# Recurrence on quarters of the array, u tiles two steps ahead, a third one-hot buffer: one change to a two-layer encoder on one core

## The chip, the core and the metric

The kernel runs on one core of a Trainium2 chip. The core has five engines that work side by side: TensorE (in profiles PE, and PEld for its weight loads), VectorE (DVE), ScalarE (ACT), GpSimd (POOL) and SyncE (SP), and 16 DMA engines. Each engine takes its instructions in the order in which the program issues them and waits on semaphores for what other engines must have done. The metric is the device time of one execution in microseconds. The number that counts is the median of several runs, and beside it stands one execution that the hardware profiler recorded.

## What is computed

Two residual layers over 512 tokens of 1,024 channels, everything in fp32. Layer 0 mixes with stick-breaking attention and pooling; layer 1 mixes with forgetting attention and with a recurrence; after each mixer comes an expert layer. Two parts matter here.

The recurrence has 8 heads of width 64:

```python
def step(state, inp):
    r_t, w_t, k_t, v_t, kk_t, a_t = inp
    sa = jnp.einsum('bhvk,bhk->bhv', state, kk_t)
    state = (state * w_t[:, :, None, :] - sa[..., None] * (kk_t * a_t)[:, :, None, :]
             + v_t[..., None] * k_t[:, :, None, :])
    y = jnp.einsum('bhvk,bhk->bhv', state, r_t)
    return state, y
```

The expert layer has 16,384 experts, each with one vector u and one vector v. Every token chooses 16 of them in each of 8 heads:

```python
s1 = jnp.einsum('thd,nd->thn', q[:, :, 0], sub_k1); v1, i1 = lax.top_k(s1, PEER_TOPK)
...
top_s, pos = lax.top_k(cand.astype(jnp.float32), PEER_TOPK)
gate = jax.nn.softmax(top_s, axis=-1)
act = jax.nn.gelu(jnp.einsum('thkd,td->thk', expert_u[ib], xb), approximate=False)
out = jnp.einsum('thk,thkd->td', gate * act, expert_v[ib])
```

## The kernel before

`build` runs `even_mixer`, `peer` (layer 0), `odd_mixer`, `peer` (layer 1). The order of the work on each engine is the order in which the Python code issues it; generators are advanced by hand to weave one piece of work into another. Nothing reorders it later. A tile that is taken again from a pool of `bufs` buffers waits until the last user of the buffer's former tile is done.

**The recurrence** (end of `odd_mixer`, lines 1094 to 1275) works on 8 chunks of 64 tokens. Within a chunk the recurrence is written as matrix products, with the inverse of a 64x64 triangular matrix for every head. The 8 heads are held as 4 pairs: partitions 0 to 63 carry one head of the pair, 64 to 127 the other. `expand` (line 718) spreads such a pair into a 128x128 block whose two diagonal quarters are the two heads and whose other quarters are zero, by multiplying with a mask; it runs on POOL, for chunk 0 partly on VectorE and ScalarE. `mm4` (line 1114) multiplies four such blocks, one for each pair, into one PSUM bank. `prep(c)` (line 1118) makes, for one chunk, the expanded operands, completes the inverse `XT` from 16 to 32 to 64 rows (masks `level`, products with N1 and N2), and turns k, b and v. It needs nothing of the state and is woven in as the preparation of the next chunk. `step(c)` (line 1187) has the chain that goes from state to state: psT, evicted as t1 by ScalarE; psU, evicted as u; psS, which with the decayed old state `se` makes the new state on VectorE, one operation for each pair; psY, the output. `group_norm(g)` (line 1227) norms two finished chunks with products of full 128x128 blocks, in six pieces woven into the steps of chunks 2 to 7 (the last of it after the loop). The last line of the loop for chunk c drains what is left of the preparation of c+1.

The stage before it computes, between the projections for the attention, the products of `gram` (line 729), one chunk at a time, with an expanded block on one side.

**The expert layer** (`peer`). TensorE multiplies every expert's u with 384 of the 512 tokens and keeps only what the gates choose; the other 128 tokens gather their experts' rows with DMAs. The u matrix comes in 128 tiles of 128 experts. `u_fetch` (line 1358) issues the DMA on SP into one of three buffers `ur`; `u_load` (line 1363) fetches two and makes the high part `uh` on ScalarE; `u_low` (line 1372) makes the low part `ul` on VectorE; `u_mm` (line 1379) does the 24 products (lines 182 to 184 in `mm3`) and the GELU. The first 15 activations stay in the on-chip memory (`NB_ACT`), the next 38 (`NB_SPILL`) are written to HBM and read again by `a_load`. While queries are projected (`for m in range(16)`), the first three tiles are loaded and two of them split, from m = 10 on.

Then `background()` issues the top-16 search and the gates: for every block of 16 tokens VectorE compares and multiplies one-hot rows `ohC`, `ohA` and two `ohB` (line 1606), and `flush` lets TensorE multiply them (line 1589). A block's last flush stands on TensorE behind the operations for the block two later. Costs are added up, and whenever they reach `G_STEP`, `u_step` (line 1626) is issued:

```python
def u_step(j):
    u_low(j + 1)
    u_load(j + 2)
    u_mm(j, j >= NB_ACT)
```

After the gates come the last u products before the v products; then a loop over the 128 v tiles, which first reads spilled activations and, from j = `NB_SPILL` on, does the remaining u products one a turn.

Of the kernel before, what the change touches and what calls it, by code (L numbers as in the profile page):

```python
# [25 lines left out]
P = 128  # L26
# [67 lines left out]
for _nm, _c in (("blk64", 128), ("mB", 128), ("mK", 256), ("lv16", 128), ("lv32", 128), ("hm", 2), ("rows", 4)):  # L94
    OC[_nm] = (_n, _c)
    _n += _c
# [3 lines left out]
def odd_const_array():  # L100
# [12 lines left out]
    put("mK", np.concatenate([same & (rr < qq), same & (rr <= qq)], 1))  # L113
    put("lv16", same & (rr // 32 == qq // 32) & (rr % 32 < 16) & (qq % 32 >= 16))
    put("lv32", same & (rr < 32) & (qq >= 32))
    put("hm", np.stack([i < 64, i >= 64], 1))
# [550 lines left out]
def odd_mixer(k):  # L667
# [8 lines left out]
    with ExitStack() as st:  # L676
# [40 lines left out]
        hm = o_("hm")  # L717

        def expand(e, dst, src):

            if e is nc.scalar:
                for h in range(2):
                    k.act(dst[:, :, 64 * h:64 * h + 64], src, AF.Copy, scale=hm[:, h:h + 1])
                return
            e.tensor_tensor(dst.rearrange("p a (h t) -> p a h t", h=2), src[:, :, None, :].to_broadcast([P, 4, 2, 64]),
                            hm[:, None, :, None].to_broadcast([P, 4, 2, 64]), op=ALU.mult)

        def gram(c, pb):
            tt = slice(64 * c, 64 * c + 64)
            b0 = pb.tile([P, 4, P], F32, name="b0", tag="b0", bufs=2)  # L730
            expand(nc.gpsimd, b0, be[:, :, tt])

            def rest():
                ps = bank4()
                for p in range(4):
                    mm(ps[:, p, :], b0[:, p, :], AR[:, p, :, tt], start=True, stop=True, skip_group_check=True)
                for p in range(4):
                    nc.vector.tensor_tensor(Na[:, :, :, 4 * c + p].rearrange("p i b -> p b i"),
                                            ps[:, p, 0:64].rearrange("p (b i) -> p b i", b=4),
                                            o_("mB")[:, 0:64].rearrange("p (b i) -> p b i", b=4), op=ALU.mult)  # L740
                nc.vector.tensor_tensor(Nr[:, c], ps[:, :, 64:], o_("mB")[:, None, 64:].to_broadcast([P, 4, 64]), op=ALU.mult)
# [5 lines left out]
        with ExitStack() as s1:  # L747
# [136 lines left out]
            with ExitStack() as s2:  # L884
# [40 lines left out]
                def grams(n):  # L925
                    if n >= 4:
                        gq.pop(0)()
                    if 2 <= n < 10:
                        gq.append(gram(n - 2, p3))
# [28 lines left out]
        def bc4(a):  # L958
            return a[:, None, :].to_broadcast([P, 4, P])

# [150 lines left out]
        def t4(nm, n=1, bufs=2):  # L1111
            return pw.tile([P, 4, n * P], F32, name=nm, bufs=bufs)

        def mm4(ps, l, r, start, stop):
            for p in range(4):
                mm(ps[:, p, :], l[:, p, :], r[:, p, :], start=start and p == 0, stop=stop, skip_group_check=True)  # L1116

        def prep(c):
            tt = slice(64 * c, 64 * c + 64)
            K0, B0 = t4("k0"), t4("b0")  # L1120
            AR0 = t4("ar", 2)
            X, XT = t4("x"), t4("xt")
            N1, N2 = t4("n1"), t4("n2", bufs=1)
            NB2 = t4("nb2")

            def level(dst, nm):
                for h in range(2):
                    f = slice(64 * h, 64 * h + 64)
                    (nc.vector if h and not c else nc.gpsimd).tensor_tensor(dst[:, :, f].rearrange("p a (b i) -> p a b i", b=4),
                                            Na[:, :, :, 4 * c:4 * c + 4].rearrange("p i b a -> p a b i"),  # L1130
                                            o_(nm)[:, None, f].rearrange("p a (b i) -> p a b i", b=4)
                                            .to_broadcast([P, 4, 4, 16]), op=ALU.mult)

            ve, ae = (nc.gpsimd, nc.gpsimd) if c else (nc.vector, nc.scalar)
            level(N1, "lv16")
            expand(ve, X, Xc[:, 4 * c:4 * c + 4, :])
            expand(ae, K0, ka[:, :, tt])
            expand(ve, XT, XTc[:, 4 * c:4 * c + 4, :])
            expand(nc.gpsimd, B0, be[:, :, tt])
            yield  # L1140
            expand(ae, AR0[:, :, 0:P], AR[:, :, 0, tt])
            level(N2, "lv32")
            expand(ve, NB2, Nr[:, c])
            expand(nc.gpsimd, AR0[:, :, P:], AR[:, :, 1, tt])
            KT, NT, VT = t4("kt"), t4("nt"), t4("vt")
            ps = bank4()
            for p in range(4):
                for s in range(2):
                    mm(ps[64 * s:64 * s + 64, p, :], vT[:, p, tt], ident, start=True, stop=True, skip_group_check=True)
            nc.vector.tensor_tensor(VT, ps, bc4(cst(k, "blk")), op=ALU.mult)  # L1150

            KK = t4("kk", 2)
            ps = bank4()
            for p in range(4):
                mm(ps[:, p, :], K0[:, p, :], AR[:, p, :, tt], start=True, stop=True, skip_group_check=True)
            for i in range(2):
                nc.vector.tensor_tensor(KK[:, :, i * P:i * P + P].rearrange("p a (h t) -> p a h t", h=2),
                                        ps[:, :, None, 64 * i:64 * i + 64].to_broadcast([P, 4, 2, 64]),
                                        o_("mK")[:, None, i * P:i * P + P].rearrange("p a (h t) -> p a h t", h=2)
                                        .to_broadcast([P, 4, 2, 64]), op=ALU.mult)  # L1160
            ps = bank4()
            mm4(ps, N1, X, True, True)
            Q = t4("q")
            k.act(Q, ps, AF.Copy)
            yield
            ps, ps2 = bank4(), bank4()
            mm4(ps, XT, Q, True, True)
            nc.vector.tensor_tensor(X, X, ps, op=ALU.subtract)
            mm4(ps2, Q, XT, True, True)
            nc.vector.tensor_tensor(XT, XT, ps2, op=ALU.subtract)  # L1170
            yield
            ps = bank4()
            mm4(ps, N2, X, True, True)
            Q = t4("q")
            k.act(Q, ps, AF.Copy)
            for src, dst, sgn in ((K0, KT, 1.0), (B0, NT, -1.0)):
                ps = bank4()
                for p in range(4):
                    nc.tensor.transpose(ps[:, p, :], src[:, p, :], ident)
                k.act(dst, ps, AF.Copy, scale=sgn)  # L1180
            yield
            ps = bank4()
            mm4(ps, Q, XT, True, True)
            nc.vector.tensor_tensor(XT, XT, ps, op=ALU.subtract)
            C[c] = (AR0, KK, KT, NT, VT, XT, NB2)

        def step(c):
            AR0, KK, KT, NT, VT, XT, NB2 = C.pop(c)
            tt = slice(64 * c, 64 * c + 64)
            s0 = S.get(c - 1)  # L1190
            psT = bank4()
            mm4(psT, KK[:, :, 0:P], VT, True, c == 0)
            if c:
                mm4(psT, AR0[:, :, 0:P], s0, False, True)
            t1 = t4("t1", bufs=1)
            k.act(t1, psT, AF.Copy)
            psS, psY = bank4(), bank4()
# [853 lines left out]
```

## Time and profile before

| | us |
|---|---|
| median of 3 runs | 3352.92 |
| lowest and highest run | 3352.59, 3361.28 |
| profiled execution | 3354.57 |
| its span | 3352.8 |
| first gates with u products, 405 to 685 | 280 |
| recurrence, 1861 to 1990 | 129 |
| second gates with u products, 2172 to 2451 | 279 |

A page of the profile gives for each engine the time in which it was busy, and groups of instructions by line, operation and tile. Matmul records are pipelined, so the time from one start to the next is the pace, not the duration of one record; an fp32 product is two records. "128\*128 128x512" reads: a stationary operand of 128 rows and 128 columns, and a moving operand of 128 partitions with 512 columns. In a bracket stands how long the engine was idle before an instruction and what ended that. Lists in order of time merge equal instructions that follow each other. A view of busy time in stretches gives for each stretch its length, the busy time and count of each engine, the granted clock of TensorE as a share of full speed (PEclk), the share of DMA time and the GB/s.

### The profile page before, as it was taken

The numbers are of one execution on the slowest core, as the hardware profiler recorded it, in microseconds if no ns is written. First come the engines' busy times: TensorE is split into PE (matmuls) and PEld (weight loads), VectorE is DVE, ScalarE is ACT, GpSimd is POOL, SyncE is SP. The second block draws the span as 40 slices with busy tenths as digits, with TensorE's granted clock in tenths as the row PEclk, the third lists the DMA queues.
The fourth block names the chain that finished last, engine by engine and source line by source line (L and its number), as shares of the span: only waits on it lengthen the run. The fifth ranks groups of instructions, "written<-read, shape, count | busy, mean of one in ns | idle before, by whom it ended". The sixth has DMA issues, their size and how long they took to land.

```text
span 3352.8 us, 53012 instructions
## 1 busy us (share of the span) xinstructions
PE 3195.3 (95%) x20560; PEld 2795.9 (83%) x20560; DVE 2462.0 (73%) x4771; ACT 1435.1 (43%) x1998; POOL 990.4 (30%) x785
## 2 busy tenths in 40 slices
PE   7999989999999999998999998989989999999998
PEld 5777888888899999986776897888877899999997
DVE  5246888957788888887565466788957788888886
ACT  3353357743333333334445334357743333333334
POOL 1004200013344444443122634200013344444442
PEclk9999999999999999999999999999999999999999
DMA  8524246699999999994520014246789999999984
GB/s 314 189 104 132 89 137 223 230 307 331 314 347 332 325 329 347 330 315 166 185 73 23 4 45 147 93 134 221 238 289 317 316 342 338 328 323 340 340 315 167
DMA packets 317117, 791.10 MB, mean 236 GB/s; under 512 B 23744, under 2 KB 158272, under 8 KB 304576
## 3 DMA queue, kind: packets, MB, share of 16 engines
q1 hardware_dynamic: 222416, 437.95, 38.2%
q0 software_dynamic: 75008, 274.78, 23.5%
q10 hardware_dynamic: 19440, 74.98, 6.0%
q8 instruction: 161, 2.64, 0.3%
q14 instruction: 92, 0.75, 0.1%
HBM read 713.92 MB, written 73.66 MB: 235 GB/s over the span
## 4 chain that ended last, share of the span: by engine, by line
PE 78%; DVE 9%; DMA 5%; ACT 5%; issue 2%; ACTq 0%; POOL 0%; SPq 0%; DVEq 0%; POOLq 0%
PE o L1701 27%; PE ups L184 9%; PE ups L182 9%; PE ups L183 9%; PE bk L1116 3%; PE bk L182 3%; PE bk L184 3%; PE bk L183 3%; DMA vr<-peer_vp 2%; PE qps L182 2%; PE qps L183 2%; PE qps L184 2%; DVE ul L1376 1%; PE gps L1589 1%; PE adaps L242 1%
## 5 line engine op out<-in xcount | busy, mean ns | idle before, releaser
L184 PE MATMUL ups<-phh,ul 128*128 128x384 f32 x2048 | 697.3, 340 | 48.9 <-DVE ul L1376 48.8
L182 PE MATMUL ups<-phh,uh 128*128 128x384 f32 x2048 | 699.0, 341 | 5.8 <-ACT acts L151 5.8
L1723 POOL DMA_INDIRECT row<-peer_u,xres x256 | 350.1, 1368 | 1173.8 <-PE gps L1589 604.3
L183 PE MATMUL ups<-phl,uh 128*128 128x384 f32 x2048 | 691.9, 338 | 0.0
L151 ACT ACTIVATE vh<-vr 128x1024 fp32r<-128x1024 f32 x254 | 269.7, 1062 | 545.3 <-issue 433.9
L1701 PE MATMUL o<-vh,Hh 128*128 128x512 f32 x1524 | 475.6, 393 | 18.3 <-ACT Hh L151 18.3
L1701 PE MATMUL o<-vh,Hl 128*128 128x512 f32 x1524 | 472.4, 391 | 0.0
L1701 PE MATMUL o<-vl,Hh 128*128 128x512 f32 x1524 | 472.3, 391 | 0.0
L1723 POOL DMA_INDIRECT row<-peer_v,xres x256 | 340.3, 1329 | 409.8 <-DVE xres L1739 314.3
L184 PEld LDWEIGHTS ups<-phh,ul 128*128 128x128 f32 x2048 | 389.6, 190 | 58.8 <-DVE ul L1376 58.8
L176 DVE TENSOR_TENSOR vl<-vr,vh 128x1024 fp32r<-128x1024 f32 x254 | 311.1, 1225 | 125.1 <-ACT vh L151 112.8
L182 PEld LDWEIGHTS ups<-phh,uh 128*128 128x128 f32 x2048 | 390.1, 191 | 12.3 <-ACT acts L151 6.4
L183 PEld LDWEIGHTS ups<-phl,uh 128*128 128x128 f32 x2048 | 389.7, 190 | 5.8
L1701 PEld LDWEIGHTS o<-vh,Hh 128*128 128x128 f32 x1524 | 282.8, 188 | 73.7 <-ACT Hh L151 25.7
L1701 PEld LDWEIGHTS o<-vl,Hh 128*128 128x128 f32 x1524 | 286.8, 188 | 62.8
L1701 PEld LDWEIGHTS o<-vh,Hl 128*128 128x128 f32 x1524 | 286.8, 188 | 61.8
L1376 DVE TENSOR_TENSOR ul<-ur,uh 128x1024 fp32r<-128x1024 f32 x256 | 312.0, 1219 | 26.5 <-ACT uh L151 17.9
L1742 DVE SCALAR_TENSOR_TENSOR gacc<-row,xres,gacc 128x1024 f32<-128x1024 f32 x256 | 327.7, 1280 | 2.3 <-DMA row<-peer_v,xres 1.6
L176 DVE TENSOR_TENSOR Hl<-Hf,Hh 128x384 fp32r<-128x384 f32 x254 | 141.9, 559 | 234.5 <-ACT Hh L151 234.5
L1739 DVE SCALAR_TENSOR_TENSOR xres<-row,xres 128x1024 f32<-128x1024 f32 x256 | 311.9, 1218 | 3.0 <-DMA row<-peer_u,xres 3.0
L151 ACT ACTIVATE uh<-ur 128x1024 fp32r<-128x1024 f32 x256 | 269.6, 1053 | 17.5 <-ACT acts L151 3.2
L151 ACT ACTIVATE act<-ups 128x384 f32<-128x384 f32 x180 | 88.5, 492 | 386.3 <-PE ups L184 386.2
(487 smaller groups left out, 4831.1 us busy)
## 6 DMA issues: line engine op xcount, KB each, us to landing
ur<-peer_uT SPq DMA_DIRECT2D x256, 512.0 KB
vr<-peer_vp SPq DMA_DIRECT2D x256, 512.0 KB
gt<-gd SPq DMA_DIRECT2D x32, 1536.0 KB
adaw<-ada_w SPq DMA_DIRECT2D x32, 1024.0 KB
wraw<-peer_wq SPq DMA_DIRECT2D x32, 512.0 KB
wraw<-od_w_in SPq DMA_DIRECT2D x30, 512.0 KB
ad<-acts ACTq DMA_DIRECT2D x76, 192.0 KB
act<-ad SPq DMA_DIRECT2D x76, 192.0 KB
```

Of the source, the lines that this page charges most:

```text
L151: return self.nc.scalar.activation(out, in_, func, **kw)
L176: (eng or k.nc.vector).tensor_tensor(lo, src, hi.bitcast(F32), op=ALU.subtract)
L182: mm(out, w[0], x[0], start=start, stop=False, skip_group_check=True)
L183: mm(out, w[0], x[1], start=False, stop=False, skip_group_check=True)
L184: mm(out, w[1], x[0], start=False, stop=stop, skip_group_check=True)
L242: nc.tensor.matmul(ps[32 * q:32 * q + 32], k.cact[:, d:d + 1].to_broadcast([P, 32]), w[:, d, q], start=d == 0, stop=d == KD - 1, skip_grou ...
L1116: mm(ps[:, p, :], l[:, p, :], r[:, p, :], start=start and p == 0, stop=stop, skip_group_check=True)
L1376: nc.vector.tensor_tensor(l, r, h.bitcast(F32), op=ALU.subtract)
L1701: mm(O_[t][b], w[:, ts], v[:, 512 * b:512 * b + 512], start=s, stop=e, skip_group_check=True)
L1723: nc.gpsimd.indirect_dma_start(out=r, out_offset=None, in_=I[f"peer_{kind}{layer}"], in_offset=bass.IndirectOffsetOnAxis(ap=eidx[:, c:c + ...
L1739: nc.vector.scalar_tensor_tensor(junk, r, 1.0, htok, op0=ALU.mult, op1=ALU.mult, accum_out=dots[:, c:c + 1])
L1742: nc.vector.scalar_tensor_tensor(acc, r, wts[:, c:c + 1], acc, op0=ALU.mult, op1=ALU.add)
```

## The change

Three parts, taken together.

The recurrence and the gram products no longer use expanded blocks. `heads` multiplies, for each head, 64 rows by 64 columns: one head on the upper left quarter of the array, the next on the lower right, both into the same PSUM bank on their own partitions. Preparation is done for two chunks at once (8 pairs of heads side by side), so it runs four times and not eight, with its four pieces spread over the first four pieces of the steps of two chunks. X and XT are updated in place, the masks are made by VectorE alone, and the transposes become ordinary products with the identity. The new state is the sum of psS and the old state, then multiplied by the decay: two VectorE operations over all pairs. Y has a tile of its own, and one eviction of 256 columns takes the place of two on 64 partitions.

In the expert layer `u_low` and `u_load` run one tile further ahead, with a fourth `uh` and a third `ul`; loading begins at m = 8 and three tiles are split before the gates. `NB_ACT` goes from 15 to 13 and `NB_SPILL` from 38 to 40. `ohA` has a third buffer.

```diff
+        def heads(ps, l, r, start=True, stop=True):
+            for a in range(ps.shape[1]):
+                for g in range(2):
+                    h = slice(64 * g, 64 * g + 64)
+                    mm(ps[h, a, :], l(h, a), r(h, a), start=start and a == 0, stop=stop, skip_group_check=True)
+        def of(t, a0=0):
+            return lambda h, a: t[h, a0 + a]
-        def gram(c, pb):
-            b0 = pb.tile([P, 4, P], F32, name="b0", tag="b0", bufs=2)
-            expand(nc.gpsimd, b0, be[:, :, tt])
+        def gram(c):
-                for p in range(4):
-                    mm(ps[:, p, :], b0[:, p, :], AR[:, p, :, tt], start=True, stop=True, skip_group_check=True)
+                heads(ps, lambda h, p: be[h, p, tt], lambda h, p: AR[h, p, :, tt])
...
+        Y = pn.tile([P, 4, T], F32, name="y")
-        Y = AR[:, :, 1]
...
-        def prep(c):
...
+        def prep(m):
+            a0 = 8 * m
+            def tt(a):
+                c = 2 * m + a // 4
+                return slice(64 * c, 64 * c + 64)
+            def level(nm):
+                n = t8(nm, bufs=1)
+                nc.vector.tensor_tensor(n.rearrange("p a (b i) -> p a b i", b=4),
+                                        Na[:, :, :, a0:a0 + 8].rearrange("p i b a -> p a b i"),
+                                        o_(nm)[:, None, :].rearrange("p a (b i) -> p a b i", b=4)
+                                        .to_broadcast([P, 8, 4, 16]), op=ALU.mult)
+                return n
+            def turned(src, sgn, nm):
+                ps = bank8()
+                heads(ps, lambda h, a: src[h, a % 4, tt(a)], lambda h, a: ident[h, h])
+                t = t8(nm)
+                k.act(t, ps, AF.Copy, scale=sgn)
+                return t
+            X, XT = Xc[:, a0:a0 + 8, :], XTc[:, a0:a0 + 8, :]
+            N1 = level("lv16")
+            ps = bank8()
+            heads(ps, of(N1), of(X))
+            Q = t8("q")
+            k.act(Q, ps, AF.Copy)
+            VT = turned(vT, 1.0, "vt")
             yield
+            ps, ps2 = bank8(), bank8()
+            heads(ps, of(XT), of(Q))
+            heads(ps2, of(Q), of(XT))
+            nc.vector.tensor_tensor(X, X, ps, op=ALU.subtract)
+            N2 = level("lv32")
+            nc.vector.tensor_tensor(XT, XT, ps2, op=ALU.subtract)
+            KT = turned(ka, 1.0, "kt")
+            yield
+            KK = t8("kk", w=P)
             for i in range(2):
+                ps = bank4()
+                heads(ps, lambda h, p: ka[h, p, tt(4 * i)], lambda h, p: AR[h, p, :, tt(4 * i)])
+                nc.vector.tensor_tensor(KK[:, 4 * i:4 * i + 4], ps, o_("mK")[:, None, :].to_broadcast([P, 4, P]), op=ALU.mult)
+            ps = bank8()
+            heads(ps, of(N2), of(X))
+            Q = t8("q")
             k.act(Q, ps, AF.Copy)
             yield
+            NT = turned(be, -1.0, "nt")
+            ps = bank8()
+            heads(ps, of(Q), of(XT))
             nc.vector.tensor_tensor(XT, XT, ps, op=ALU.subtract)
...
         def step(c):
...
+            psT = half()
+            heads(psT, lambda h, p: KK[h, a0 + p, 0:64], of(VT, a0), True, c == 0)
             if c:
+                heads(psT, lambda h, p: AR[h, p, 0, tt], of(s0), False, True)
...
-                nc.vector.tensor_tensor(se, s0, ec[:, :, c:c + 1].to_broadcast([P, 4, P]), op=ALU.mult)
...
-                for p in range(4):
-                    nc.vector.scalar_tensor_tensor(s1[:, p, :], psS[:, p, :], ec[:, p, c:c + 1], se[:, p, :],
-                                                   op0=ALU.mult, op1=ALU.add)
+            if c:
+                nc.vector.tensor_tensor(s1, psS, s0, op=ALU.add)
+            nc.vector.tensor_tensor(s1, s1 if c else psS, ec[:, :, c:c + 1].to_broadcast([P, 4, 64]), op=ALU.mult)
             S[c] = s1
...
         for c in range(8):
-            nx = prep(c + 1) if c < 7 else iter(())
+            if c % 2 == 0 and c < 6:
+                nx = prep(c // 2 + 1)
...
-            drain(nx)
+            if c % 2:
+                drain(nx)
...
-NB_ACT = 15
-NB_SPILL = 38
+NB_ACT = 13
+NB_SPILL = 40
...
-                h = up.tile([P, KD, P], F32R, name="uh", bufs=3)
+                h = up.tile([P, KD, P], F32R, name="uh", bufs=4)
...
-                l = up.tile([P, KD, P], F32R, name="ul")
+                l = up.tile([P, KD, P], F32R, name="ul", bufs=3)
...
-                if m in (10, 12, 14):
-                    u_load(m // 2 - 5)
-                if m in (11, 13):
-                    u_low(m // 2 - 5)
+                if m in (8, 10, 12, 14):
+                    u_load(m // 2 - 4)
+                if m in (9, 11, 13):
+                    u_low(m // 2 - 4)
...
-                C, A = (wk.tile([P, GB // 2, P, 2], F16, name=nm, bufs=n) for nm, n in (("ohC", 1), ("ohA", 2)))
+                C, A = (wk.tile([P, GB // 2, P, 2], F16, name=nm, bufs=n) for nm, n in (("ohC", 1), ("ohA", 3)))
...
         def u_step(j):
-            u_low(j + 1)
-            u_load(j + 2)
+            u_low(j + 2)
+            u_load(j + 3)
             u_mm(j, j >= NB_ACT)
```

The same two lines change in the loop over the v tiles.

More of the change, by code (lines that the diff above doesn't have):

```diff
@@ L93 @@
 _n = 0
-for _nm, _c in (("blk64", 128), ("mB", 128), ("mK", 256), ("lv16", 128), ("lv32", 128), ("hm", 2), ("rows", 4)):
+for _nm, _c in (("blk64", 128), ("mB", 128), ("mK", 128), ("lv16", 64), ("lv32", 64), ("rows", 4)):
     OC[_nm] = (_n, _c)
@@ L928, in grams @@
                     if 2 <= n < 10:
-                        gq.append(gram(n - 2, p3))
+                        gq.append(gram(n - 2))
                 late = None
@@ L1164, in prep @@
             k.act(Q, ps, AF.Copy)
             yield
[L1166 to L1180, printed above, removed]
@@ L1204, in step @@
             yield
-            psU = bank4()
-            mm4(psU, XT, t1, True, True)
-            u = t4("u", bufs=1)
+            psU = half()
+            heads(psU, of(XT, a0), of(t1))
+            u = t8("u", 4)
             k.act(u, psU, AF.Copy)
             if c:
-                mm4(psY, s0, AR0[:, :, P:], False, False)
+                heads(psY, of(s0), lambda h, p: AR[h, p, 1, tt], False, False)
             yield
-            mm4(psS, NT, u, False, True)
-            s1 = t4("S")
@@ L1214, in step @@
-            if c == 0:
-                nc.vector.tensor_tensor(s1, psS, ec[:, :, c:c + 1].to_broadcast([P, 4, P]), op=ALU.mult)
-            else:
-                for p in range(4):
-                    nc.vector.scalar_tensor_tensor(s1[:, p, :], psS[:, p, :], ec[:, p, c:c + 1], se[:, p, :],
-                                                   op0=ALU.mult, op1=ALU.add)
+            heads(psS, of(NT, a0), of(u), False, True)
+            s1 = t8("S", 4)
+            if c:
+                nc.vector.tensor_tensor(s1, psS, s0, op=ALU.add)
@@ L1220, in step @@
+            nc.vector.tensor_tensor(s1, s1 if c else psS, ec[:, :, c:c + 1].to_broadcast([P, 4, 64]), op=ALU.mult)
             S[c] = s1
-            mm4(psY, u, NB2, False, True)
-            for s in range(2):
-                h = slice(64 * s, 64 * s + 64)
-                k.act(Y[h, :, tt], psY[h, :, 64 * s:64 * s + 64], AF.Copy)
+            heads(psY, of(u), lambda h, p: Nr[h, c, p], False, True)
+            k.act(Y[:, :, tt], psY, AF.Copy)
             yield
@@ L1671, in v_load @@
                     h, l = (up.tile([P, KD, P], F32R, name=nm, bufs=b).rearrange("p a b -> p (a b)")
[L1672 removed]
+                            for nm, b in (("uh", 4), ("ul", 3)))
                 else:
```

99 lines of the change are left out of this document (21 added, 78 removed).

## The prediction

> **What bounds the kernel now.** I read the page first (busy time, then the chain that ended last), then busy time by stage, then the instructions in order of time in the two stages that the diff touches, then the waits there.
>
> ```profile
> span 3352.8 us, 53012 instructions
> PE 3195.3 (95%) x20560; PEld 2795.9 (83%) x20560; DVE 2462.0 (73%) x4771; ACT 1435.1 (43%) x1998; POOL 990.4 (30%) x785
> PE 78%; DVE 9%; DMA 5%; ACT 5%; issue 2%; ACTq 0%; POOL 0%; SPq 0%; DVEq 0%; POOLq 0%
> ```
>
> TensorE (PE) is busy 95% of the span and holds 78% of the chain, so time is won by giving it less work or by ending its pauses. The stages, by the busy time in each stretch:
>
> ```profile
> core 0: us, PE busy (x) PEld busy (x) DVE busy (x) ACT busy (x) POOL busy (x), PEclk, DMA share, GB/s
> 295.00:405.00 110.00, 110.00 (x1047) 94.81 (x1046) 82.78 (x528) 37.96 (x53) 39.32 (x24) 1.00 0.39 116
> 405.00:685.00 280.00, 253.28 (x1887) 242.64 (x1886) 246.55 (x551) 182.72 (x208) 0.00 (x0) 0.96 0.58 194
> 685.00:718.00 33.00, 27.15 (x136) 25.85 (x136) 9.29 (x10) 14.57 (x19) 4.92 (x5) 0.90 1.03 360
> 1861.00:1990.40 129.40, 127.18 (x1127) 123.23 (x1128) 70.21 (x120) 41.89 (x81) 80.77 (x82) 0.97 0.04 13
> 2172.00:2451.00 279.00, 252.28 (x1895) 241.59 (x1894) 246.43 (x551) 183.70 (x208) 0.75 (x1) 0.98 0.58 196
> ```
>
> 295 to 405 is the queries of the first expert layer, 405 to 685 its gates with the u products between them, 685 to 718 the passage to the v products, 1861 to 1990 the recurrence, 2172 to 2451 the second gates. The recurrence is pure TensorE: 127.2 of 129.4 us. In the gates neither engine is full: TensorE pauses 26.7 us, VectorE (DVE) 33.4 us.
>
> **The recurrence.** One chunk of TensorE's order, and the first and last product after the first preparation:
>
> ```profile
> 1872.85 1.06 PE L1116 MATMUL bk<-vt,kk 128*128 128x128 f32 x8
> 1901.12 1.06 PE L1116 MATMUL bk<-vt,kk 128*128 128x128 f32 x8
> 1902.02 1.06 PE L1116 MATMUL bk<-S,ar 128*128 128x128 f32 x8
> 1905.59 1.06 PE L1116 MATMUL bk<-ar,S 128*128 128x128 f32 x8
> 1906.58 1.09 PE L1149 MATMUL bk<-consts,xres 128*64 128x128 f32 x16
> 1907.60 1.16 PE L1155 MATMUL bk<-AR,k 128*128 128x128 f32 x8
> 1908.59 1.06 PE L1116 MATMUL bk<-x,n 128*128 128x128 f32 x8
> 1917.65 1.06 PE L1116 MATMUL bk<-vt,kk 128*128 128x128 f32 x8
> 1989.62 1.06 PE L1255 MATMUL bk<-xg,lwg 128*128 128x128 f32 x8
> ```
>
> A product is two records, a group of four products 8 records, and the next group starts 0.89 us later: 111.6 ns a record, with no gap. A chunk takes 16.5 us (1901.12 to 1917.65). From 1872.85 to the last group's end at about 1990.4 are 117.6 us. The transposes of v (L1149) write the two column halves in turn: 16 records in 1.09 us, less the last one's 0.28, are 54.3 ns each, half of 111.6; going there costs 0.10 us more than a group (1905.59 to 1906.58) and coming back 0.15 (1.02 less 16 times 54.3 ns).
>
> After, every 128x128 block with two heads on its diagonal becomes two 64x64 products on opposite quarters, moving 64 columns where 128 moved: twice the records. What a record costs decides all. No row shows two opposite quarters at once; the nearest are the 32-column strips of the conditioning products:
>
> ```profile
> 1597.33 1.10 PE L242 MATMUL adaps<-Na,cact 128*32 128x64 f32 x64
> 319.45 0.76 PE L242 MATMUL adaps<-nx,cact 128*32 128x32 f32 x64
> L242 PE MATMUL adaps<-Na,cact x256: 219/219/243, 1597.3 to 1640.3; 128*32 128x64 f32 x128
> ```
>
> Less the tail of 0.22, 64 columns on four strips take 14.0 ns a record: 56 ns in each strip, four at a time. Two quarters at once with 64 columns give 28 ns. The bounds: 27 below (half of 54.3); above, 56 if the quarters take turns, and 219, one whole record (third row), if each must end before the next starts. I take 28, because the row with the same width shows it; 31 if a wider load counts.
>
> The Trainium skill (TensorEngine Tiling, Restrictions and Gotchas) speaks against it: different row tiles cannot access the same PSUM bank at the same time, and each pair here writes one bank, on different partitions. The strips above share a bank at full pace, but not from different rows, so this is open; by the rule the sum would be that of the third rival.
>
> By pairs of chunks, as the new loop goes: the steps have 8 groups of four head pairs a chunk, 16 records of 28 ns, 0.45 us each, 7.2 us a pair of chunks. Preparation has 8 groups of 32 records, 0.90 each, and two products with kappa that still move 128 columns, 16 records of 54.3 ns, 0.87 each: 8.9 us. The group norm keeps three groups of 128x128, 0.89 plus 0.25 for going and coming: 3.4 us. First pair (no group norm, chunk 0 without its two state groups): 15.2. Second and third: 19.5 each. Fourth (no preparation): 10.6. Sum 65 us.
>
> The eviction waits must then be covered by less:
>
> ```profile
> L151 ACT ACTIVATE t<-bk 128x512 f32<-128x512 f32 x8 | 4.8, 595 | 11.8 <-PE bk L1116 11.8
> L151 ACT ACTIVATE AR<-bk 64x256 f32<-64x256 f32 x16 | 6.0, 378 | 8.4 <-PE bk L1116 8.4
> L1168 DVE TENSOR_TENSOR x<-x,bk 128x512 f32<-128x512 f32 x8 | 5.5, 686 | 4.1 <-PE bk L1116 4.1
> L1218 DVE SCALAR_TENSOR_TENSOR S<-bk,ec,se 128x128 f32<-128x128 f32 x28 | 7.9, 343 | 2.4 <-PE bk L1116 2.0
> L1129 DVE TENSOR_TENSOR n<-Na,oc x2: 605/893/1181, 1861.5 to 1864.7; 128x256 f32<-128x256 f32 x2
> ```
>
> Evictions of t1 and u shrink from 595 ns to about 378 (256 columns). The state becomes an add and a multiply of 256 columns, each between 343 and 686 ns, about 0.42, so 0.84 in a row where four operations took 4 x 0.28 (busy 7.9 over 28); the product se goes. The chain of a chunk is three groups (1.35), two evictions (0.76), 0.84, and six hand-overs of about 0.25 (a group ends 0.17 after its pace, 1.06 less 0.89, and a semaphore): 4.5 us. An even chunk has some 10 us of TensorE work around it, an odd one 5, with nothing prepared during its last two thirds: there u and the state wait 0.5 to 1 us each unless a group-norm group lies between. I allow 6 us of stalls, 3 to 12. VectorE's new work a pair, two masks of about 1.2, five operations of 0.69 and four of 0.42, is 7.5 us, with 5 of group norm well under 19.5; ScalarE has about 8. POOL's 80.8 us of expansions go; TensorE hardly waited for them, so that alone buys nothing. The first preparation now makes two chunks with one 1.2 us mask ahead: its chain is about 12 us against 11.3 (1861.5 to 1872.85): +1.
>
> So 65 + 6 + 1 = 72 for 117.6: **-45 us** (-52 with 27 ns and few stalls, -34 with 31 and many). The gram products of the stage before go to quarters with 128 columns, 0.87 against 0.89 a group, and pay 0.25 for the switch eight times: +2 at most. SP's and POOL's queues lose nothing but POOL's operations here.
>
> **The gates.** The waits from 405 to 685, TensorE's and VectorE's, and one instance:
>
> ```profile
> PE ups L184 <- DVE ul L1376: 20.7, 13, 4.1
> PE gps L1589 <- DVE ohB L1606: 5.3, 4, 1.8
> DVE ohA L1606 <- PE gps L1589: 23.4, 11, 5.1
> DVE ul L1376 <- ACT uh L151: 4.5, 3, 1.9
> ...
> 466.48 1.55 PE L1589 MATMUL gps<-ohB,ohA 128*128 128x128 f16 x24
> 467.15 1.23 DVE L1606 TENSOR_TENSOR ohA<-xres,pT 128x2048 f16<-128x2048 f16 x1 [5.08 <-PE gps L1589]
> 469.89 1.22 DVE L1376 TENSOR_TENSOR ul<-ur,uh 128x1024 fp32r<-128x1024 f32 x1
> 471.17 0.69 PE L184 MATMUL ups<-phh,ul 128*128 128x384 f32 x1 [2.73 <-DVE ul L1376]
> 712.06 0.56 DVE L1682 TENSOR_TENSOR Hf<-act,gt 128x384 f32<-128x384 f32 x1 [4.01 <-DMA gt<-gd]
> ```
>
> They hold each other up: VectorE stands 5.08 us for a one-hot buffer that TensorE frees only behind a u product; behind ohA stands the low part ul, and so TensorE then stands 2.73. With ul made one product earlier, its 20.7 us go wherever it was late by less than one product; the longest wait was 4.1. The third ohA lets VectorE pass; but ohB keeps four buffers, two a block, so the wait comes back at the first ohB, one operation of 1.2 us or more later, where the work between hides it. What is late next is VectorE itself: 246.6 us of work and 5 of waits for ScalarE in 280 leave at most 28, TensorE's 253.3 at most 26.7; the 5.3 for ohB stay. One product of slack does not level everything: I take 15 us a layer, 5 to 24, **-30** for both.
>
> The first load and split of u move two queries ahead; ScalarE's 38 and VectorE's 82.8 of 110 busy us hide them (1.22 for a split, as the ul row, and no more for a load), and the 512 KB on SP go at a DMA share of 0.39; uncovered they would cost 2.4 a layer. In the passage one more u tile is under way (512 KB at 360 GB/s, 1.5 us), and the first v product waits for the gates to come back (Hf at 712.06) anyway: 0, +2 a layer at most. Two products more are spilled; the number of products and the lead of each buffer stay: 0.
>
> **The sum.** The profiled execution took 3354.57 us, 1.8 around its span, and lies 1.65 over the median of 3352.92. 3354.6 - 45 - 30 + 2 = 3281.6; against the median **3280 us**.
>
> **The rivals.** One: the gates do not gain, because VectorE is the bound and the waits only move to ohB; for it speak its 246.6 us, against it that both engines pause at once. 3354.6 - 45 + 2 - 2 = 3310.
>
> Two: the clock. With smaller groups and the same evictions TensorE's load falls and the clock halves in the recurrence. The passage shows a granted 0.90 with 27 of 33 us busy, the recurrence 0.97. Then 65 becomes 130 and stalls vanish: +13, +2, less 30: 3338. The Trainium skill (TensorE: Matmul & The Clock Gate, HAM oscillation) says that gaps of some 3 us bring the half clock; my gaps are under 1 us, so by that rule too it is unlikely.
>
> Three: the quarters take turns, 56 ns. A pair of chunks is then 14.3 + 17.8 + 3.4 (12.5 + 17.8 the first, 17.7 the last), sum 119; the first preparation grows by 6, the gram products by 9: +16, less 30: 3339.
>
> Four, slower than before: a quarter waits for the other's product to leave the array before it writes the same bank. About 2,500 records of 64 columns (992 in steps, 1,024 in preparation, the wider ones counted twice) make every ns worth 2.5 us, so from 61 ns a record on the gain of the gates is eaten. At 111.6, the pace of a full record, it is (111.6 - 56) x 2.5 = 139 more than rival three: 3478. The strips of L242 speak against it.
>
> **Chances.** Forecast 0.70 (its own range 3258 to 3300), rival one 0.13, two 0.05, three 0.06, four 0.06. Within 0.3% (10 us) is about what a measurement here cannot tell from no change. Faster by more: forecast, rival one and half of two and three, 0.88; same 0.06; slower 0.06. The range from 3258 to 3325 holds the forecast and rival one, some eight tenths.
>
> **What would show it.** In the recurrence: records of form 64*64 every 28 ns (a group of 32 in some 0.9 us plus tail), no POOL work, last lwg group about 45 us sooner after the first mask, clock 0.95 or more. In the gates: TensorE's wait for ul under 5 us, VectorE's wait for gps shorter and named at ohB, each stretch near 265 us. I am wrong if a group of 32 records takes over 1.2 us, if stalls on u or S pass 12 us, or if the gates stay within 5 us of 280.

## The result

The changed kernel takes 3267.47 us (median of 4 runs, 3267.38 to 3272.05) beside 3352.76 for the kernel before (4 runs, 3351.36 to 3361.28): a ratio of 0.9744, 95% interval 0.9726 to 0.9762, or 85 us less. The forecast was 3280 with a range of 3258 to 3325. The profiled execution took 3267.50, against 3354.57 before; its span is 87.1 us shorter.

The page of the changed kernel: span, busy time, shares of the chain that ended last.

```profile
span 3265.7 us, 55046 instructions
PE 3133.8 (96%) x21696; PEld 2739.4 (84%) x21696; DVE 2429.3 (74%) x4725; ACT 1419.4 (43%) x1974; POOL 893.2 (27%) x696
...
PE 80%; DVE 9%; DMA 5%; ACT 4%; issue 3%; SPq 0%; ACTq 0%; DVEq 0%
```

Only 61.5 us of TensorE's busy time went (3195.3 to 3133.8); the other 26 us are pauses that ended. The stages that answer to those of the prediction, by busy time in each stretch:

```profile
core 0: us, PE busy (x) PEld busy (x) DVE busy (x) ACT busy (x) POOL busy (x), PEclk, DMA share, GB/s
295.00:402.00 107.00, 107.00 (x1029) 91.70 (x1027) 80.54 (x505) 37.37 (x52) 38.86 (x24) 1.00 0.38 124
402.00:658.00 256.00, 247.20 (x1910) 240.04 (x1909) 248.63 (x575) 184.72 (x210) 0.00 (x0) 0.99 0.61 214
658.00:690.00 32.00, 25.37 (x128) 24.10 (x127) 7.98 (x8) 13.66 (x17) 5.83 (x5) 0.92 1.02 360
1842.00:1925.60 83.60, 78.70 (x2217) 76.02 (x2218) 40.24 (x75) 28.95 (x58) 0.59 (x1) 1.00 0.07 22
2103.00:2360.00 257.00, 248.13 (x1909) 240.86 (x1908) 248.65 (x575) 184.37 (x210) 0.00 (x0) 0.99 0.61 213
```

In the gates the same work now fits in 256 and 257 us where it had 283 and 281. In the recurrence the clock is full in this execution and POOL is idle. To say where each microsecond went, I put marks at the starts of TensorE's products: the last score product, the last gate product, the first and last v product of a layer, the last attention product (L1011), the last lwg product (that of the fourth group norm, which runs among the output products some 14 us behind the loop). Between marks, in us:

| stretch | before | after | difference |
|---|---|---|---|
| gates, first layer (401.2 to 684.7; 401.9 to 657.5) | 283.5 | 255.6 | -27.9 |
| to the first v product | 29.6 | 29.6 | 0 |
| v products, first layer | 854.6 | 862.3 | +7.7 |
| to the last attention product | 290.1 | 290.5 | +0.4 |
| recurrence, and on to the last lwg | 145.5 | 99.6 | -45.9 |
| to the last score product of the second layer | 163.7 | 163.5 | -0.2 |
| gates, second layer | 281.0 | 256.8 | -24.2 |
| to the first v product | 30.5 | 29.4 | -1.1 |
| v products, second layer | 857.8 | 861.3 | +3.5 |
| ahead of the first mark, behind the last | 416.5 | 417.1 | +0.6 |

The sum is -87.1. In both layers' gates TensorE does the same 1,906 records before and after. Busy time between the marks of the gates, first before, then after (columns as above):

```profile
401.20:684.70 283.50, 256.78 (x1907) 246.14 (x1906) 250.04 (x575) 183.97 (x209) 0.00 (x0) 0.96 0.57 191
2168.20:2449.20 281.00, 254.28 (x1907) 243.59 (x1906) 249.93 (x575) 183.90 (x209) 0.00 (x0) 0.98 0.57 193
```

```profile
401.90:657.50 255.60, 246.80 (x1908) 239.64 (x1907) 248.74 (x575) 184.32 (x210) 0.00 (x0) 0.99 0.61 214
2103.00:2359.80 256.80, 247.93 (x1908) 240.66 (x1907) 248.65 (x575) 184.17 (x210) 0.00 (x0) 0.99 0.61 213
```

TensorE's pauses fall from 26.7 us to 8.8 and 8.9. The rest of what the gates win, 10 and 6 us, is TensorE's own busy time, at a granted clock that rose from 0.96 and 0.98 to 0.99.

Now TensorE in order of time at the start of the recurrence, at the first step, and at the end:

```profile
1843.39 1.15 PE L723 MATMUL bk<-Xc,lv 64*64 64x64 f32 x32 [3.18 <-DVE lv L1121]
1844.38 1.10 PE L723 MATMUL bk<-consts,xres 64*64 64x64 f32 x32
1845.31 1.10 PE L723 MATMUL bk<-q,XTc 64*64 64x64 f32 x32
...
1852.65 0.63 PE L723 MATMUL bk<-vt,kk 64*64 64x64 f32 x16
1853.12 0.63 PE L723 MATMUL bk<-vt,kt 64*64 64x64 f32 x16
...
1922.24 0.68 PE L723 MATMUL bk<-t,XTc 64*64 64x64 f32 x16 [0.88 <-ACT t L151]
1922.75 0.63 PE L723 MATMUL bk<-AR,S 64*64 64x64 f32 x16
1923.40 0.68 PE L723 MATMUL bk<-u,nt 64*64 64x64 f32 x16
1923.92 0.63 PE L723 MATMUL bk<-Nr,u 64*64 64x64 f32 x16
1924.48 1.16 PE L1232 MATMUL bk<-xg,lwg 128*128 128x128 f32 x8
```

A group of 32 records starts 0.93 us after the one before: 29.1 ns a record. TensorE's waits in that stage, the first mask `lv` ahead of all others:

```profile
PE bk L723 <- DVE lv L1121: 5.3, 3, 3.2
PE bk L723 <- ACT t L151: 0.9, 1, 0.9
PE bk L1218 <- ACT sqy L151: 0.4, 1, 0.4
```

And the waits in the first gates (402 to 658), TensorE's and VectorE's:

```profile
PE gps L1568 <- DVE ohB L1585: 4.4, 5, 1.0
PE pkT L1545 <- DVE pk L1479: 2.9, 1, 2.9
...
DVE ul L1355 <- ACT uh L151: 3.6, 2, 3.5
```

TensorE's 20.7 us for `ul` and VectorE's 23.4 us at `ohA` are gone altogether. VectorE has 248.6 us of work in the 256 and waits for TensorE nowhere.

### The profile page after: what moved, and what is told of

It is laid out like the page before. It is cut to its first block, busy times and chain, and to the rows that moved or that the text cites. A ratio compares the mean times of both kernels' runs of the same rounds, so it can differ in the third digit from the quotient of the medians.

```text
span 3265.7 us, 55046 instructions
## 1 busy us (share of the span) xinstructions
PE 3133.8 (96%) x21696; PEld 2739.4 (84%) x21696; DVE 2429.3 (74%) x4725; ACT 1419.4 (43%) x1974; POOL 893.2 (27%) x696
## 4 chain that ended last, share of the span: by engine, by line
PE 80%; DVE 9%; DMA 5%; ACT 4%; issue 3%; SPq 0%; ACTq 0%; DVEq 0%
PE o L1680 27%; PE ups L182 9%; PE ups L184 9%; PE ups L183 9%; PE bk L182 3%; PE bk L184 3%; PE bk L183 3%; DMA vr<-peer_vp 2%; PE bk L723 2%; PE qps L182 2%; PE gps L1568 2%; PE qps L183 2%; PE qps L184 2%; PE adaps L242 1%; DVE ul L1355 1%
## 5 line engine op out<-in xcount | busy, mean ns | idle before, releaser
L184 PE MATMUL ups<-phh,ul 128*128 128x384 f32 x2048 | 689.9, 337 | 0.0
```

The lines of the kernel that those rows point to most:

```text
L184: mm(out, w[1], x[0], start=False, stop=stop, skip_group_check=True)
```

## Experiments

Each group of runs stands beside runs of the kernel before on the same chip. "Gates" are the two stretches of the table.

**Which part brings what.** Three kernels with one part alone, and the change without its third ohA. Kernel before took 3353.66 us beside them (3348.44 to 3364.04).

The recurrence and the gram products alone (`uh`, `ul`, `ohA`, `NB_ACT`, `NB_SPILL` and the calls of `u_load` and `u_low` as before; the edit in short):

```diff
-("ohA", 3)   NB_ACT = 13, NB_SPILL = 40   uh bufs=4   ul bufs=3   u_low(j + 2); u_load(j + 3)
+("ohA", 2)   NB_ACT = 15, NB_SPILL = 38   uh bufs=3   ul bufs=2   u_low(j + 1); u_load(j + 2)
```

> Only the recurrence and the gram products are changed; loads and splits of u, the spills and the one-hot buffers are as before. Independent parts: between the last attention product and the last gate product of the recurrence's loop 131 us become 85, as in the changed kernel, and nothing else moves: 3352.8 - 46 = 3307 us, 3304 to 3310. Parts that help each other (the shorter recurrence brings the second gates forward or the memory lies differently): off that by more than 3 us.

Measured: 3318.17 us, ratio 0.9884 (0.9859 to 0.9909). The recurrence has 101.0 us for 145.5 (-44.5); TensorE's waits for `ul` (48.3 us in the whole kernel) and VectorE's at `ohA` (48.2) stay as they were. The term of the recurrence stands. The whole is 11 us above the 3307 expected, more than the 3 us that were to tell independent parts from parts that help each other. In the trace the excess lies in small additions (gates 285.1 and 281.0, v products 857.3 and 862.1) in stages where nothing was touched, so a difference of 2 to 5 us in a stretch says little of an edit; whether the parts help each other by a few us stays open.

The u tiles ahead alone, on the kernel before (in short; the earlier loads among the queries belong to it):

```diff
-u_low(j + 1); u_load(j + 2)   uh bufs=3   ul bufs=2   NB_ACT = 15, NB_SPILL = 38
+u_low(j + 2); u_load(j + 3)   uh bufs=4   ul bufs=3   NB_ACT = 13, NB_SPILL = 40
```

> The kernel before with u split two steps ahead, the fourth uh, the third ul and 13 + 40 activations; two ohA buffers. Theory (two waits of their own): TensorE's waits for ul in the gates, 20.7 us a layer, fall under 3, VectorE's waits at ohA, 23.4, stay over 10; 8 to 12 us a layer are gained: 3330 to 3338 us. Rival (lockstep: VectorE stood for TensorE only because TensorE had stood for ul): both waits fall under 4, the whole 20 us a layer come from this part: 3308 to 3316 us.

The third ohA alone, on the kernel before:

```diff
-for nm, n in (("ohC", 1), ("ohA", 2))
+for nm, n in (("ohC", 1), ("ohA", 3))
```

> The kernel before with only the third ohA buffer. Theory (two waits of their own): VectorE's wait moves to ohB and shrinks by a half or more, 4 to 9 us a layer are gained: 3335 to 3345 us. Rival (lockstep): nothing or under 2 us a layer, since TensorE still stands for ul and ohB waits in ohA's place: 3349 to 3353 us.

The changed kernel with two ohA (the same line turned back):

> The changed kernel with two ohA buffers in place of three. Theory (two waits of their own): VectorE's waits at ohA come back, 10 us or more a layer, and 8 to 12 us a layer are lost: 3283 to 3292 us. Rival (lockstep): 3267 to 3270 us, as changed.

Measured:

| kernel | us | ratio (95%) | gates |
|---|---|---|---|
| u ahead alone | 3313.72 | 0.9876 (0.9850 to 0.9903) | 263.3, 263.6 |
| third ohA alone | 3318.89 | 0.9880 (0.9849 to 0.9910) | 262.4, 263.7 |
| changed kernel, two ohA | 3274.53 | 0.9759 (0.9732 to 0.9787) | 264.4, 262.2 |

Either edit alone takes some 20 us from the first gates and 17 from the second; both together 28 and 24. So neither of my two theories held (the time of u ahead alone lies in the rival's range, the other two in no range): the two waits are not separate (20 + 20 would be 40), and the third ohA is not idle beside the u tiles. What is left of the waits between the two engines from 402 to 666 (who waited for whom: us, times, longest), first with u ahead alone, then with the third ohA alone:

```profile
PE gps L1589 <- DVE ohB L1606: 8.7, 6, 2.7
DVE ohA L1606 <- PE gps L1589: 6.6, 3, 3.5
```

```profile
PE ups L184 <- DVE ul L1376: 7.9, 7, 4.1
PE gps L1589 <- DVE ohB L1606: 4.1, 4, 1.7
DVE ohB L1606 <- PE gps L1589: 2.4, 2, 1.5
```

With u ahead VectorE's wait at ohA falls from 23.4 to 6.6 us although ohA still has two buffers; with the third ohA TensorE's wait for `ul` falls from 20.7 to 7.9 although `ul` is made no earlier. It was one cycle: VectorE waits for a buffer that TensorE frees behind a u product, and that u product waits for the `ul` behind VectorE's wait. Cut at either point, most of both waits ends.

**Is VectorE the bound of what is left?** Two runs that take work from VectorE in the gates. First 13 of the 48 `ul` a layer on GpSimd (kernel before beside it: 3355.74 us):

```diff
-u_low(j + 2)
+u_low(j + 2, nc.gpsimd if j % 3 == 1 and j < 40 else nc.vector)
```

> 13 of the 48 ul subtractions a layer in the gates go from VectorE to GpSimd, which has no work there. Theory: with both edits of the change in place VectorE is the bound of the gates (248.6 us busy of 256.0); without 13 x 1.22 = 16 us it has 233, TensorE with 247 us busy is next, and the stretch from the last score product to the last gate product is 249 to 252 us, 4 to 7 less a layer. What is won may be given back in part in the v loop: time 3255 to 3266 beside about 3266 for after. Rival: GpSimd's 2.5 us for one ul (the row of 128x1024 subtractions on GpSimd) slows VectorE beside it or comes late for TensorE; then the stretch is 256 to 265 us and TensorE waits for ul again.

Measured: 3279.04 us, 0.9763 (0.9746 to 0.9780); gates 261.3 and 261.2, longer than the 256 of the changed kernel. The rival came, within its 256 to 265 us for the stretch: VectorE is slowed, though TensorE does not wait for `ul`. VectorE's groups from 402 to 658 (line, engine, operation, tiles, shapes, count; busy, mean ns; idle before), in the changed kernel and then here:

```profile
L1585 DVE TENSOR_TENSOR ohB<-ohC,pT 128x2048 f16<-128x2048 f16 x48 | 57.6, 1219 | 0.1
L1585 DVE TENSOR_TENSOR ohA<-xres,pT 128x2048 f16<-128x2048 f16 x24 | 29.2, 1218 | 0.0
```

```profile
L1585 DVE TENSOR_TENSOR ohB<-ohC,pT 128x2048 f16<-128x2048 f16 x47 | 62.8, 1356 | 0.0
L1585 DVE TENSOR_TENSOR ohA<-xres,pT 128x2048 f16<-128x2048 f16 x24 | 35.3, 1472 | 0.0
```

One instance, VectorE and GpSimd in order of time:

```profile
463.57 4.56 DVE L1585 TENSOR_TENSOR ohB<-ohC,pT 128x2048 f16<-128x2048 f16 x2
468.05 1.21 DVE L1514 TENSOR_TENSOR m<-c,d1x 128x2048 f16<-128x2048 f16 x1
```

```profile
463.74 3.31 POOL L1355 TENSOR_TENSOR ul<-ur,uh 128x1024 fp32r<-128x1024 f32 x1 [12.63 <-ACT uh L151]
```

GpSimd starts while the first ohB runs, and ends at 467.05; the second ohB ends one operation of 1.2 us behind that, give or take 0.1 us. The two operations of VectorE take 4.5 us where they take 2.3: GpSimd's 2.4 us (what one `ul` takes there when nothing holds it up) stand between them as if on one engine. Over the whole stretch (401 to 663) GpSimd is busy 37.1 us, of which some 31 are its own work (13 times 2.4), and VectorE is busy 256.3, where 248.6 less 13 times 1.22 would be 232.7: 23.6 us were added for 15.9 taken away. The Trainium skill (SBUF — State Buffer, section on the two separate sides of SBUF) has the rule: a VectorE operation with two inputs in SBUF and a GpSimd operation that reads SBUF lock each other out for the whole instruction. In this instance the trace agrees.

So this run could not answer its question. The second leaves work out instead (kernel before beside it: 3359.27 us):

```diff
-nc.vector.tensor_tensor(l, r, h.bitcast(F32), op=ALU.subtract)
+n = KD // 2 if j < 50 else KD
+nc.vector.tensor_tensor(l[:, 0:n], r[:, 0:n], h[:, 0:n].bitcast(F32), op=ALU.subtract)
...
-mm3(k, ps[:, :TD], (h[:, d, :], l[:, d, :]), ...)
+mm3(k, ps[:, :TD], (h[:, d, :], (l if j >= 50 or d < KD // 2 else h)[:, d, :]), ...)
```

> Kernel after, but for the first 50 u tiles of a layer only half of the low part ul is computed, and the products of the other half take the high part in its place: TensorE's records stay, VectorE has 48 operations of about 0.65 us in the gates in place of 1.22, some 27 us less. (So that half of the low products is not what it should be; this run only asks which engine sets the pace.) Theory: VectorE is the bound of the gates after the change; TensorE, busy 247 us, is next, and the stretch from the last score product to the last gate product is 249 to 252 us, 4 to 7 less a layer, with TensorE's waits for ohB near 2 us. Rival: what is left of the pauses comes from the order of the work (ohB's four buffers, pk and pT at the head of each group of tokens), not from VectorE's load; then it stays at 255 to 257 us.

Measured: 3255.62 us, 0.9691 (0.9663 to 0.9719); gates 250.4 and 251.1. Busy time, and VectorE's first two waits from 402 to 660:

```profile
402.00:654.00 252.00, 247.49 (x1919) 241.26 (x1918) 225.17 (x580) 184.44 (x211) 0.00 (x0) 0.99 0.64 218
```

```profile
DVE ohB L1586 <- PE gps L1569: 13.0, 9, 3.3
DVE ul L1356 <- ACT uh L151: 8.2, 3, 4.0
```

VectorE has 25 us less of `ul` (58.5 us become 33.4), the stretch ends 5.2 and 5.7 us sooner, and now VectorE waits for TensorE, at ohB, where it never waited in the changed kernel. VectorE is the bound after the change, with TensorE 5 us behind it.

**What the quarters' pace rests on.** The changed kernel with all products of one quarter in a row, then all of the other (kernel before beside this and the next two edits: 3355.52 us, 3349.98 to 3362.47; the changed kernel once more: 3265.64, 0.9728, 0.9711 to 0.9745):

```diff
-for a in range(ps.shape[1]):
-    for g in range(2):
+for g in range(2):
+    for a in range(ps.shape[1]):
```

> The changed kernel with the order of the 64x64 products turned: first all products of a group on the upper left quarter, then all on the lower right. Theory: the 29 ns a record come from two quarters at work at once, and records of one quarter that follow each other take turns: about 55 ns a record, a group of 32 in 1.8 us; from the last attention product to the last output product of the recurrence 99.6 us become 155 to 165, the whole 3325 to 3335 us. Rival: 29 ns is the pace at which TensorE takes small records, whichever quarter they go to: 3266 to 3273 us.

Measured: 3303.56 us (2 runs), 0.9845 (0.9822 to 0.9867), between the two ranges; from the last attention product to the last lwg 133.0 us, against 101.1 in the changed kernel beside it. TensorE at the start, and later; then the clock of the start, here and in the changed kernel beside it (columns as in the table of stages):

```profile
1853.78 0.36 PE L723 MATMUL bk<-q,XTc 64*64 64x64 f32 x1
...
1856.46 0.36 PE L723 MATMUL bk<-XTc,q 64*64 64x64 f32 x1
...
1868.85 0.27 PE L723 MATMUL bk<-XTc,q 64*64 64x64 f32 x1
...
1870.36 0.27 PE L723 MATMUL bk<-vt,kk 64*64 64x64 f32 x1
1870.41 0.22 PE L723 MATMUL bk<-XTc,q 64*64 64x64 f32 x1
...
1870.93 0.27 PE L723 MATMUL bk<-vt,kt 64*64 64x64 f32 x1
```

```profile
1850.00:1864.00 14.00, 14.00 (x164) 14.00 (x163) 2.33 (x3) 1.79 (x3) 0.00 (x0) 0.50 0.01 1
```

```profile
1842.00:1845.00 3.00, 3.00 (x62) 3.00 (x60) 0.00 (x0) 1.20 (x2) 0.00 (x0) 0.50 0.00 0
```

Within a run on one quarter the records start 58 ns apart at full clock (single records between 1869.07 and 1869.60), twice the 29.1 of the alternating order. Yet a group of 32 takes 1.51 us (1868.85 to 1870.36), 47 ns a record, and a group of 16 takes 0.57, 36 ns: at each change of quarter a few records of the new run start between the last ones of the old (1870.36, 1870.41). 1,024 records at 18 ns more and 992 at 7 make 25 us. The other 7 are the clock: from 1849.6 to 1866 it is 0.50, a group takes 2.68 us, and 16.4 us of it would take 9.2 at 1.51. So the pace comes from two quarters that run at once. Both write one PSUM bank, on different partitions, and no cost of that shows: 29.1 is half of 58.

The clock halves at this place in the changed kernel too, but for less time. In the repeat beside this run it is 0.50 for 3.4 us from 1841.9, shortly behind the 3.2 us for which TensorE waits for the first mask, and the recurrence takes 101.1 us for 99.6; the execution shown in the result kept the full clock behind the same pause. In all five other executions on record with that pause and the alternating order the clock is 0.50 for 3.4 us, as in the repeat. Why the clock stays down for 17 us when the quarters come in runs, with TensorE busy throughout, is open.

**The first mask.** Masks `lv` of the next pair at the end of the preparation before, the first one during the attention of two heads earlier:

```diff
-N1 = level("lv16")
+N1 = N1s.pop(m)
...
+if m < 3:
+    N1s[m + 1] = level("lv16", m + 1, t8("lv16", bufs=1))
```

> The changed kernel with the first mask of a pair of chunks made earlier: that of the first pair during the last attention heads, the others at the end of the pair before. TensorE's waits for lv (5.3 us in three places, 3.2 the longest) go. Theory (TensorE is the bound of the recurrence): 4 to 5 us less than the changed kernel, 3262 to 3264. Rival (the next wait, for X, Q or the state, takes their place): under 1.5 us less.

Measured: 3259.42 us, 0.9712 (0.9696 to 0.9729). From the last attention product to the last lwg 95.0 us for 101.1, and TensorE's wait for `lv` is 0.4 us:

```profile
PE bk L723 <- ACT t L151: 0.9, 1, 0.9
...
PE bk L723 <- DVE lv L959: 0.4, 1, 0.4
```

The stretch shows 6 us: 4.9 of waits for `lv`, and the clock, which without the pause stays full here and costs 1.5 us in the kernel beside it. The times themselves hardly tell the two kernels apart (3255.29 to 3266.75 here, 3259.67 to 3268.72 there).

**What the v products give back.** Two theories for the 7.7 and 3.5 us: DMA traffic at the head of the v loop, and the two products more that are spilled. The first, by fewer gathered rows during the tiles that also load spilled activations:

```diff
-units = [0 if j < 4 else 2.5 if j < NB_SPILL else ...
+units = [0 if j < 4 else 1.0 if j < NB_SPILL else ...
```

> The changed kernel with fewer gathered rows worked off while spilled activations are read (weight 1.0 in place of 2.5 for the v tiles 4 to 39, the rest later). Theory: the gates' gain is partly given back because the first 40 v tiles are bound by DMA (TensorE's waits for Hh 13.6 us there in the first layer, 3.7 before the change): with fewer rows these waits fall under 7 us, and 5 to 8 us a layer are gained: 3252 to 3260. Rival: the waits come from the order of the reads on SP, not from their amount: 3266 to 3270; or the rows are missed later in the tail: slower than 3270.

Measured: 3252.31 us, 0.9694 (0.9679 to 0.9710); v products 850.2 and 852.7 us, where the changed kernel beside it has 859.6 and 859.5. Busy time from 690 to 860, first in the changed kernel, then here (columns as in the table of stages; TensorE's is the third, DMA share and GB/s are the last two):

```profile
690.00:860.00 170.00, 161.66 (x695) 132.17 (x693) 119.45 (x170) 60.18 (x77) 48.77 (x30) 0.98 0.90 303
```

```profile
690.00:860.00 170.00, 169.71 (x745) 140.32 (x744) 108.84 (x152) 65.88 (x84) 24.13 (x14) 0.99 0.82 266
```

TensorE pauses 8.3 us in the first and 0.3 in the second. What is late in the first are the v tiles, for whose DMA ScalarE waits before it makes their high part (same stretches, first the changed kernel, then here):

```profile
ACT vh L151 <- DMA vr<-peer_vp: 14.8, 4, 4.9
```

```profile
ACT vh L151 <- DMA vr<-peer_vp: 2.6, 2, 1.5
```

So the rows' transfers hold up those of the v tiles. The second theory, 13 and 40 on the kernel before:

```diff
-NB_ACT = 15
-NB_SPILL = 38
+NB_ACT = 13
+NB_SPILL = 40
```

> Kernel before with 40 tiles of activations stored and loaded back in place of 38, and two fewer kept. Theory: the two more cost nothing of their own: both stretches of v products stay within 2 us of 854.6 and 857.8, the time is that of the kernel before within 3 us. Rival: the two more loads are what lengthens the v loop by 8 and 4 us in after: 862 and 861, TensorE's waits for Hh go from 18 to about 30 us, and the time is 8 to 16 us above the kernel before.

Measured: 3361.49 us (10 runs) beside 3355.74 (14), 1.0017 (1.0002 to 1.0031); v products 859.7 and 855.2, waits for `Hh` 20.7. That is +5.1 in the one layer and -2.6 in the other: neither theory's numbers, an effect between nothing and 0.3%. Without that edit the v products of the kernel with quarters alone took 857.3 and 862.1. So a few us of the 11 may be the spills, a few the spread between executions; this stays open. A sooner end of the gates is at most a small part of it: with the third ohA alone the gates are 21 and 17 us shorter, and the v products take 856.4 and 860.5. In the first layer all kernels with 13 and 40 (but for those with the later rows) take 859.6 to 864.3, those with 15 and 38 take 854.6 to 857.3; in the second layer the two kinds overlap. What is shown is that the head of the loop is held up by DMA. That was so before the change: in the 170 us behind the first v product TensorE paused 3.7 us in the first layer and 6.9 in the second, at 313 and 305 GB/s.

**The two together.** Masks early and rows later in one kernel:

> The two edits of masks_early and gather_later together. Theory: they lie in different stages (the recurrence, the v loop) and add up: 6 us sooner at the last product of lwg, 7 to 9 us a layer shorter v loops; against a kernel before of about 3355 the time is 3244 to 3250, ratio 0.967 to 0.969. Rival: both only move the start of the same v loop, and what one gives the other takes back; then it is 3252 to 3258 as gather_later was alone.

Measured: 3246.13 us (3243.51 to 3249.29), 0.9667 (0.9652 to 0.9682). 94.9 us from the last attention product to the last lwg, v products 848.9 and 851.6: they add up. That is 3.3% under the kernel before, where the changed kernel is 2.6% under it; it is the fastest of all that ran.

## Why the prediction was right, and where it was off

| term | forecast | measured |
|---|---|---|
| record on two quarters | 28 ns (27 to 31 likely) | 29.1 |
| group of 32 records | 0.90 us | 0.93 |
| first step to the end of the loop's last lwg | 71 us for 117.6 | 72.7 |
| stalls within it | 6 us (3 to 12), on u and S | 3.4: `lv` 2.1, `t` 0.9, `sqy` 0.4 |
| first preparation | +1 | -1.1 (+0.4 in the repeat) |
| recurrence, sum | -45 | -45.9 |
| gram | +2 at most | +0.4 |
| gates, a layer | -15 (-5 to -24) | -27.9, -24.2; TensorE's pauses alone -17.9, -17.8 |
| passage | 0 | 0, -1.1 |
| v products | 0 | +7.7, +3.5 |

The **recurrence** came as worked out. The row of the strips with the same width gave the record to 1.1 ns; on some 2,000 records that is 2 us of the 69 us of products where 65 were counted. The stalls were half of those allowed and on another tile: the mask at the head of each preparation, which I had priced as VectorE's work, but as a wait only in the first preparation. It is issued only where it is needed; the run with early masks shows what that cost. Chunks with nothing prepared beside them do wait (0.88 us at 1922.24 for t1), but less than 1 us as said.

**Rivals two to four.** The clock is 1.00 in the recurrence of the execution shown and 0.50 for only 3.4 us in the repeat, worth 1.5 us; "my gaps are under 1 us" overlooked the first mask's 3.2. The quarters do not take turns and none waits for the other to drain. The rule of the Trainium skill that I weighed against the change (TensorEngine Tiling (Array Packing), Restrictions and Gotchas: different row tiles and one PSUM bank) sets no pace when the two write different partitions: 29.1 ns with a shared bank, against 47 in the order that has mostly one quarter at work.

**Rival one** fell: the waits did not move to ohB. TensorE's wait for it was 5.3 us in the first gates and is 4.4. VectorE's wait for TensorE, which the forecast too saw coming back at ohB, did not come back at all while VectorE is the busier engine; in the run with half of the low parts, where it is not, it is there with 13.0 us.

The **gates** are the step that was mis-sized: "One product of slack does not level everything: I take 15 us a layer, 5 to 24". The layers won 27.9 and 24.2, and the stretches are 256 us where I said near 265. Two things are in this. The first is the pauses, which the 15 us were meant for: they fell by 18 a layer, within the range. The instance quoted showed the cycle; what I did not see is that in a cycle either edit alone would win most (14 of the 26.7 us of pauses in both layers), so that two of them leave little but VectorE's own work: 248.6 of 256 us. I priced two partial cures of two waits instead of one cycle cut twice. The second is the clock, for which the forecast has no term here, though its table shows 0.96 in the first gates and 0.98 in the second. TensorE's busy time for the same records fell by 10 and 6 us; by the share not granted times the length, some 9 and 3 us of that are the clock (an estimate). That the clock rose because the pauses went is not tested.

The **v products** at 0 were wrong in the other direction. I had counted buffers and leads, but not that the head of that loop waits for DMA, so that its length moves with the traffic; how much of the 11 us the change itself costs is open. 22 us more in the gates and 11 less here, with 3 us of small terms, are the 14 by which the profiled execution beat the sum of 3281.6. That the total came within 13 us of 3280 is in part luck: two errors of opposite sign.

## What to carry to other kernels

Where two engines wait for each other in turn, their waits are one: price the cycle against the work of the busier engine, do not add the cuts (here either one alone ended half of TensorE's pauses, and both ended two thirds), and look whether the clock column leaves something to win as well. Where half of a 128x128 block is zeros, two 64x64 products on opposite quarters, issued in turn, run at once, and here a row that moves the same number of columns on several strips of the array gave the price of a record to 1 ns. When a stage is shortened, look at what bounds the next one: here the head of the next loop was held up by DMA, before the change and after, and moving its gathers later won another 13 us.

## What the runs showed that I had not expected

An idle GpSimd is no free help for VectorE: 37.1 us of subtractions there, GpSimd's own waits included, lengthened VectorE's operations by 23.6 us (0.64 us for each us), in the instance shown by the whole 2.4 us of the other engine's operation. And TensorE's order of issue between quarters matters beyond a group: a record that moves 64 columns costs 29.1 ns when quarters alternate, 36 or 47 in runs of 8 or 16 on one quarter, with the overlap at the runs' borders making the difference from 58. And a pause of 3.2 us ahead of the recurrence was followed by a halved clock in seven of eight executions, for 3.4 us in six of them, for 17 in the one with the quarters in runs.
